# Prompt attention: ScalarE copies the transposed blocks of both heads out of PSUM, in place of VectorE for one head and ScalarE for the other

## The chip, the core and the metric

The kernel runs on one core of a Trainium2 chip. The metric is device time in microseconds (us), the median of several runs. A core has TensorE (PE in the profile; PEld is its weight load), VectorE (DVE), ScalarE (ACT), GpSimd (POOL), and SyncE (SP), which issues all DMAs here. Each engine works through its own instructions in program order; an instruction waits on semaphores for what it needs from the others. Matmuls write to PSUM, and their results are copied from there to SBUF before they can be an operand again.

## The reference, cut to what matters

Two layers of a hybrid encoder, for one prompt of 2048 tokens and 8 short samples. Each layer has an input projection, a state-space branch, a stick-breaking attention branch (8 heads of 64) and an output projection. The change concerns the prompt's attention:

```python
z = jnp.einsum('bqhd,bkhd->bhqk', q, k) * (HEAD_DIM ** -0.5)
mask = k_pos[None, :] < q_pos[:, None]
log_1mb = jnp.where(mask, -jax.nn.softplus(z), 0.0)
after = lax.cumsum(log_1mb, axis=3, reverse=True) - log_1mb
a = jnp.where(mask, jnp.exp(jax.nn.log_sigmoid(z) + after), 0.0)
return jnp.einsum('bhqk,bkhd->bqhd', a, v)
```

## The kernel before

`attn_prompt` runs once in each layer. It loops over blocks of query tiles (four tiles of 128 queries in a block; in layer 1 the last four tiles make two blocks of two, so `nt` is 4 or 2), over four pairs of heads, and over chunks of 512 keys from the diagonal down. For each chunk, head and query tile, TensorE makes the scores `pz` (L819, L820, on the diagonal also the mask, L822), ScalarE takes their sigmoid into `u` (L824), and VectorE runs a cumulative product along the keys (L826, the scan). Then the key blocks of 128 are taken two at a time, as a group: for each block and head TensorE transposes the tiles of `u` into a PSUM bank `pt` (L838), the bank is copied to SBUF as `aT` (L840 for head 0, L841 for head 1), and TensorE multiplies it by the differences of V into `po` (L845). The first L845 of a group waits for the last copy of the group. Where a head pair is done, VectorE makes `za` from `po` (L854).

PSUM holds two `pt` banks while layer 0's attention runs and three in layer 1; of `aT` there are six buffers.

No order is written out by hand: a scheduler takes the whole program, with its own estimate of each instruction's cost, and lays out each engine's order. So attention is interleaved with other work. In layer 0 it runs beside the gated unit `glu`, the modulation matmuls (L242), the output projection (L1246 to L1248) and the input projection of layer 1 (L673 to L675, whose weights ScalarE casts in L171 and VectorE or GpSimd split in L172). In layer 1 it runs beside `glu` and the output projection. In the last microseconds of layer 1's attention that other work has run out.

Counted over the program, 376 banks are copied by each of L840 and L841: 160 pairs in layer 0 and 216 in layer 1, in 188 groups.

Of the kernel before, what the change touches and what calls it, by code (L numbers as in the profile page):

```python
# [44 lines left out]
class Trunk:  # L45
# [731 lines left out]
    def attn_prompt(self, l, blocks):  # L777
        nc = self.nc
        v, gp, sc, pe, ident = nc.vector, nc.gpsimd, nc.scalar, nc.tensor, self.ident
        with ExitStack() as es:  # L780
            ap = self.pool(es, f"a{l}{blocks[0][0]}", right=True)
            for t0, nt, hp in [(t0, nt, hp) for t0, nt in blocks for hp in range(H // 2)]:
# [17 lines left out]
                for kc in range(top, -1, -1):  # L800
                    diag = kc == top
                    nk = (t0 + nt) * 128 - kc * 512 if diag else 512
                    ks = slice(kc * 512, kc * 512 + nk)
                    V1 = ap.tile([128, 4, 128], F32, name="V1", bufs=2)
                    self.dma(V1[:, 0:nk // 128], self.dv_d[l][ks, rp].rearrange("(b p) c -> p b c", p=128))
                    As = [[], []]
                    for hh in range(2):
                        rs = slice(hp * 128 + hh * 64, hp * 128 + hh * 64 + 64)
                        K1 = ap.tile([128, 512], F32R, name="K1", bufs=3)
                        self.dma(K1[:, 0:nk], self.kT[l][rs, :, ks].rearrange("d s t -> (d s) t"))  # L810
                        Q1, Q2 = Qt[hh]
                        for i in range(nt):
                            W = (t0 + i + 1) * 128 - kc * 512 if diag else 512
                            o = 512 - W
                            pz = self.pz()
                            qi = slice(i * 128, (i + 1) * 128)
                            N = max(W, 256)
                            c0, c1 = 512 - N, 512 - N + W
                            pe.matmul(pz[:, c0:512], Q1[:, qi], K1[:, 0:N], start=True, stop=False)  # L819
                            pe.matmul(pz[:, c0:512], Q2[:, qi], K1[:, 0:N], start=False, stop=not diag)  # L820
                            if diag:
                                pe.matmul(pz[:, c1 - 128:c1], self.identb, self.maskb, start=False, stop=True)  # L822
                            u = ap.tile([128, 512], F32, name="u", bufs=16)
                            sc.activation(u[:, o:512], pz[:, c0:c1], AF.Sigmoid, scale=-0.125)  # L824
                            un = u[:, o:512][:, ::-1]
                            v.tensor_tensor_scan(un, un, un, 1.0 if diag else carry[hh * 4 + i], ALU.mult, ALU.bypass)  # L826
                            carry[hh * 4 + i] = u[:, o:o + 1]
                            As[hh].append(u)
                    for j0 in range(0, nk // 128, 2):
                        group = []  # L830
                        for j in range(j0, min(j0 + 2, nk // 128)):
                            i0 = max(0, kc * 4 + j - t0)
                            s = slice(i0 * 128, nq)
                            pTs = [self.pt(), self.pt()]
                            for hh in range(2):
                                for i in range(i0, nt):
                                    off = (512 - ((t0 + i + 1) * 128 - kc * 512)) if diag else 0
                                    pe.transpose(pTs[hh][:, i * 128:(i + 1) * 128], As[hh][i][:, off + j * 128:off + (j + 1) * 128], ident)  # L838
                            aTs = [ap.tile([128, 512], F32, name="aT", bufs=6) for _ in range(2)]
                            v.tensor_copy(aTs[0][:, s], pTs[0][:, s])  # L840
                            last = sc.copy(aTs[1][:, s], pTs[1][:, s])  # L841
                            group += [(j, s, hh, aTs[hh]) for hh in range(2)]
                        for n, (j, s, hh, aT) in enumerate(group):
                            c = slice(hh * 64, hh * 64 + 64)
                            mm = pe.matmul(po[c, s], V1[:, j, c], aT[:, s], start=diag and j == 0,  # L845
                                           stop=kc == 0 and j == 3, tile_position=(0, hh * 64))
                            if n == 0:
                                self.after(mm, last)
# [438 lines left out]
```

## Time and profile before

| | |
|---|---|
| median of 3 runs | 3225.33 us (3224.55 to 3226.41) |
| the profiled execution | 3223.93 us, span 3221.9 us |
| TensorE busy | 92% of the span |
| VectorE busy | 69% |
| ScalarE busy | 40% |
| GpSimd busy | 22% |
| mean granted TensorE clock | 0.965 of full speed |

The profiled execution's own time is 1.4 us below the median; the span is the time from the first to the last instruction in it. Busy shares are means over stages with different limits, so the stages in which the changed lines run matter. A wait is put down to the instruction that ended it, with the engine and tile that released it.

### The profile page before, as it was taken

How to read it: one execution, taken by the hardware profiler on the slowest of the kernel's cores; microseconds unless marked ns; L12 is line 12 of the kernel's file. 1: busy time of each engine (PE TensorE's matmuls, PEld its weight loads, DVE VectorE, ACT ScalarE, POOL GpSimd, SP SyncE). 2: the span in 40 equal slices, each digit the busy share in tenths (PEclk: the TensorE clock that was granted, in tenths of full speed). 3: DMA queues.
4: the chain of work that ended last, by engine and by line, in shares of the span. 5: the costliest groups of instructions: out<-in, count | busy, mean ns of one | idle time of the engine just before them, and what ended most of it. 6: DMA issues, size and time to landing. Idle time of an engine off the chain costs nothing.

```text
span 3221.9 us, 47149 instructions
## 1 busy us (share of the span) xinstructions
PE 2955.8 (92%) x16902; PEld 2268.8 (70%) x16902; DVE 2237.8 (69%) x3885; ACT 1295.2 (40%) x2646; POOL 713.4 (22%) x468
## 2 busy tenths in 40 slices
PE   6978679899988989999999998899999799999998
PEld 4756578798767666767777886677789566666665
DVE  6699774757566667577896637446574889777765
ACT  5632224334442334365443323373243345343432
POOL 1155664101302021221012103312200202111310
PEclk8989899999999999999999998899999899999999
DMA  6645554466677975343434314667764757345552
GB/s 207 169 144 171 207 175 150 134 186 180 227 258 235 300 227 156 111 157 121 130 116 157 129 65 146 228 195 216 229 192 128 240 149 230 116 129 164 188 156 74
DMA packets 516099, 555.27 MB, mean 172 GB/s; under 512 B 87203, under 2 KB 369491, under 8 KB 515098
## 3 DMA queue, kind: packets, MB, share of 16 engines
q1 hardware_dynamic: 515866, 552.26, 54.9%
q8 instruction: 134, 2.20, 0.3%
q14 instruction: 99, 0.81, 0.1%
HBM read 378.12 MB, written 169.86 MB: 170 GB/s over the span
## 4 chain that ended last, share of the span: by engine, by line
PE 61%; DVE 12%; DMA 8%; issue 4%; ACT 2%; SPq 1%; POOL 1%; DVEq 0%; ACTq 0%; POOLq 0%
PE po L845 7%; PE pt L838 7%; PE pm L673 4%; PE pm L674 4%; PE pm L675 4%; PE pz L819 3%; PE pm L1246 3%; PE pm L1247 3%; PE pz L820 3%; PE pm L1248 3%; PE pm L726 3%; DVE u L826 3%; PE pm L728 3%; PE pm L727 3%; PE pz L993 1%
## 5 line engine op out<-in xcount | busy, mean ns | idle before, releaser
L826 DVE TENSOR_TENSOR_SCAN u<-u 128x512 f32<-128x512 f32 (+3 forms) x640 | 723.0, 1166 | 65.6 <-ACT u L824 63.8
L673 PE MATMUL pm<-wH,hH 128*128 128x512 f32 x1088 | 448.9, 413 | 28.8 <-ACT kn L760 16.4
L674 PE MATMUL pm<-wL,hH 128*128 128x512 f32 x1088 | 445.1, 409 | 8.7 <-DVE wL L172 6.9
L675 PE MATMUL pm<-wH,hL 128*128 128x512 f32 x1088 | 445.9, 410 | 4.4 <-POOL hL L649 2.8
L841 ACT COPY aT<-pt 128x512 f32<-128x512 f32 (+1 forms) x376 | 175.5, 470 | 572.8 <-PE pt L838 540.7
L824 ACT ACTIVATE u<-pz 128x512 f32<-128x512 f32 (+3 forms) x640 | 321.8, 536 | 152.5 <-PE pz L820 48.2
L838 PEld LDWEIGHTS pt<-ident,u 128*128 128x128 f32 x2176 | 249.6, 141 | 174.3 <-issue 107.6
L838 PE MATMUL pt<-ident,u 128*128 128x128 f32 x2176 | 340.8, 280 | 26.6 <-DVE aT L840 19.7
L840 DVE COPY aT<-pt 128x512 f32<-128x512 f32 (+1 forms) x376 | 198.9, 533 | 231.0 <-PE pt L838 218.7
L845 PE MATMUL po<-aT,V 128*64 128x512 f32 (+1 forms) x1504 | 285.5, 497 | 12.4 <-DVE za L854 4.6
L819 PE MATMUL pz<-K,Q 128*128 128x512 f32 (+2 forms) x640 | 273.3, 427 | 4.7 <-issue 1.8
L726 PE MATMUL pm<-hH,wH 128*128 128x384 f32 (+1 forms) x768 | 260.9, 340 | 17.5 <-DVE kn L731 17.5
L728 PE MATMUL pm<-hH,wL 128*128 128x384 f32 (+1 forms) x768 | 257.6, 336 | 10.0 <-POOL wL L172 7.9
L673 PEld LDWEIGHTS pm<-wH,hH 128*128 128x128 f32 x1088 | 210.6, 194 | 79.6 <-ACT kn L760 17.5
L727 PE MATMUL pm<-hL,wH 128*128 128x384 f32 (+1 forms) x768 | 258.9, 337 | 0.0
L674 PEld LDWEIGHTS pm<-wL,hH 128*128 128x128 f32 x1088 | 210.6, 194 | 57.4 <-DVE wL L172 10.2
L675 PEld LDWEIGHTS pm<-wH,hL 128*128 128x128 f32 x1088 | 210.7, 194 | 56.9 <-POOL hL L649 6.5
L172 POOL TENSOR_TENSOR wL<-wr,wH 128x512 fp32r<-128x512 f32 x96 | 149.6, 1569 | 422.1 <-ACT wH L171 224.9
L820 PE MATMUL pz<-K,Q 128*128 128x512 f32 (+2 forms) x640 | 235.5, 368 | 0.0
L1246 PE MATMUL pm<-owH,mH 128*128 128x512 f32 x512 | 207.7, 407 | 10.6 <-DVE yt L1249 9.6
L1247 PE MATMUL pm<-owL,mH 128*128 128x512 f32 x512 | 206.2, 403 | 6.2 <-DVE owL L172 5.1
L1248 PE MATMUL pm<-owH,mL 128*128 128x512 f32 x512 | 204.2, 399 | 0.6 <-POOL mL L172 0.6
(373 smaller groups left out, 5245.8 us busy)
## 6 DMA issues: line engine op xcount, KB each, us to landing
wr<-in_w_in_dram SPq DMA_DIRECT2D x192, 256.0 KB
K<-kT SPq DMA_DIRECT2D x184, 256.0 KB
Q<-qT SPq DMA_DIRECT2D x112, 256.0 KB
wm<-in_w_mod_dram SPq DMA_DIRECT2D x24, 1024.0 KB
V<-dv_d SPq DMA_DIRECT2D x92, 256.0 KB
out_dram<-kn SPq DMA_DIRECT2D x68, 256.0 KB
qT<-x SPq DMA_DIRECT2D x64, 256.0 KB
kT<-x SPq DMA_DIRECT2D x64, 256.0 KB
```

The costliest lines, as they stand in the source:

```text
L673: pe.matmul(ps, hH[:, k, cs], wH[k], start=k == 0, stop=False)
L674: pe.matmul(ps, hH[:, k, cs], wL[k], start=False, stop=False)
L675: pe.matmul(ps, hL[:, k, cs], wH[k], start=False, stop=k == KT - 1)
L726: pe.matmul(ps[:, 0:n], wH[k][:, ws], hH[:, k, 0:n], start=k == 0, stop=False)
L727: pe.matmul(ps[:, 0:n], wH[k][:, ws], hL[:, k, 0:n], start=False, stop=False)
L728: pe.matmul(ps[:, 0:n], wL[k][:, ws], hH[:, k, 0:n], start=False, stop=k == KT - 1)
L819: pe.matmul(pz[:, c0:512], Q1[:, qi], K1[:, 0:N], start=True, stop=False)
L820: pe.matmul(pz[:, c0:512], Q2[:, qi], K1[:, 0:N], start=False, stop=not diag)
L824: sc.activation(u[:, o:512], pz[:, c0:c1], AF.Sigmoid, scale=-0.125)
L826: v.tensor_tensor_scan(un, un, un, 1.0 if diag else carry[hh * 4 + i], ALU.mult, ALU.bypass)
L838: pe.transpose(pTs[hh][:, i * 128:(i + 1) * 128], As[hh][i][:, off + j * 128:off + (j + 1) * 128], ident)
L845: mm = pe.matmul(po[c, s], V1[:, j, c], aT[:, s], start=diag and j == 0, stop=kc == 0 and j == 3, tile_position=(0, hh * 64))
```

## The change

One line: the copy of head 0's bank goes to ScalarE, which already copies head 1's.

```diff
                             aTs = [ap.tile([128, 512], F32, name="aT", bufs=6) for _ in range(2)]
-                            v.tensor_copy(aTs[0][:, s], pTs[0][:, s])
+                            sc.copy(aTs[0][:, s], pTs[0][:, s])
                             last = sc.copy(aTs[1][:, s], pTs[1][:, s])
```

The scheduler lays the program out anew. TensorE, GpSimd and SyncE issue the same instructions as before (15256, 473 and 1902; 171 of SyncE's DMAs stand a few places earlier or later), VectorE 376 fewer, ScalarE 376 more. Up to the first attention instruction of layer 0 nothing moves. The last matmuls of other work stand at the same point of layer 1's attention as before.

On VectorE, near the end of layer 1's attention (the scan is printed as SCALAR_TENSOR_TENSOR, L826), before:

```order
L826 SCALAR_TENSOR_TENSOR u<-u 128x384
L840 COPY aT<-pt 128x256
L826 SCALAR_TENSOR_TENSOR u<-u 128x512
L840 COPY aT<-pt 128x256 x4
L826 SCALAR_TENSOR_TENSOR u<-u 128x512 x4
```

and now:

```order
L826 SCALAR_TENSOR_TENSOR u<-u 128x384
L826 SCALAR_TENSOR_TENSOR u<-u 128x512
L826 SCALAR_TENSOR_TENSOR u<-u 128x384
L826 SCALAR_TENSOR_TENSOR u<-u 128x512 x13
L854 SCALAR_TENSOR_TENSOR za<-po,vE,za 128x128 x2
```

The copies that stood four in a row between four scans and the next four are gone, and 13 scans follow each other.

On ScalarE, at the same place (L824 is the sigmoid), before:

```order
L824 ACTIVATE u<-pz 128x512
L841 COPY aT<-pt 128x256 x3
L824 ACTIVATE u<-pz 128x512 x3
L841 COPY aT<-pt 128x256 x2
L824 ACTIVATE u<-pz 128x512
```

and now:

```order
L840 COPY aT<-pt 128x256
L841 COPY aT<-pt 128x256
L840 COPY aT<-pt 128x256
L841 COPY aT<-pt 128x256
L840 COPY aT<-pt 128x256
L841 COPY aT<-pt 128x256
L824 ACTIVATE u<-pz 128x512
L840 COPY aT<-pt 128x256
L824 ACTIVATE u<-pz 128x512 x2
L841 COPY aT<-pt 128x256
```

Head 0's copy stands ahead of head 1's, and in one of the pairs two sigmoids stand between the two.

On TensorE, where the second-to-last head pair ends its diagonal chunk (V_28895 is that chunk's V), before:

```order
L838 MATMUL pt<-ident,u 128x128 x8
L845 MATMUL po<-aT,V_28895 64x256 x4
L838 MATMUL pt<-ident,u 128x128 x2
L845 MATMUL po<-aT,V_28895 64x256 x2
L838 MATMUL pt<-ident,u 128x128 x2
L845 MATMUL po<-aT,V_28895 64x128 x2
```

and now:

```order
L838 MATMUL pt<-ident,u 128x128 x9
L845 MATMUL po<-aT,V_28895 64x256 x4
L838 MATMUL pt<-ident,u 128x128 x5
L845 MATMUL po<-aT,V_28895 64x256 x2
L845 MATMUL po<-aT,V_28895 64x128 x2
```

The four L845 of the second group stood in two runs with transposes between them, and now stand in one. Over the whole order 188 groups stood in 206 such runs, and now in 188.

## Rows read from the trace of the kernel before

**Rows 1.** The page: busy time, share of the span, instructions of each engine.

```profile
PE 2955.8 (92%) x16902; PEld 2268.8 (70%) x16902; DVE 2237.8 (69%) x3885; ACT 1295.2 (40%) x2646; POOL 713.4 (22%) x468
```

**Rows 2.** Stretch, busy us (count): PE, PEld, DVE, ACT, POOL; clock, DMA share, GB/s.

```profile
1030.00:1830.00 800.00, 770.83 (x4446) 557.70 (x4445) 578.91 (x956) 357.78 (x703) 124.98 (x82) 0.99 0.52 164
2570.00:3125.00 555.00, 539.30 (x3006) 380.27 (x3006) 440.40 (x546) 229.72 (x491) 104.27 (x63) 0.99 0.53 161
3125.00:3180.00 55.00, 45.39 (x296) 27.88 (x296) 44.31 (x63) 23.99 (x58) 0.00 (x0) 1.00 0.39 114
```

**Rows 3.** Groups by line and shape: busy us, mean ns | idle ahead, releasers.

```profile
L840 DVE COPY aT<-pt 128x512 f32<-128x512 f32 x172 | 117.3, 683 | 139.4 <-PE pt L838 139.0
L841 ACT COPY aT<-pt 128x512 f32<-128x512 f32 x172 | 100.7, 586 | 298.7 <-PE pt L838 295.9 <-PE pz L822 1.9
...
L840 DVE COPY aT<-pt 128x256 f32<-128x256 f32 x140 | 57.0, 413 | 63.3 <-PE pt L838 56.4 <-PE po L845 6.1
L841 ACT COPY aT<-pt 128x256 f32<-128x256 f32 x140 | 51.9, 378 | 182.3 <-PE pt L838 181.1 <-PE po L845 1.1
```

**Rows 4.** Line L840: who waited for it (us, times).

```profile
  PE pt L838: 19.7, 18
...
  PE po L845: 4.0, 2
```

**Rows 5.** Line L841: who waited for it (us, times).

```profile
  PE pt L838: 4.4, 7
  PE po L845: 3.1, 5
```

**Rows 6.** TensorE's waits, layer 0's attention: us in total, times, longest.

```profile
PE po L845 <- DVE za L854: 3.2, 3, 1.3
```

**Rows 7.** TensorE's waits, layer 1's attention to 3125 us.

```profile
PE pm L1247 <- DVE owL L172: 3.2, 3, 1.6
...
PE pm L1246 <- DVE yt L1249: 2.0, 2, 1.7
PE pt L838 <- DVE u L826: 1.6, 1, 1.6
```

**Rows 8.** TensorE's waits from 3125 to 3180 us.

```profile
PE pt L838 <- DVE aT L840: 8.0, 6, 1.4
```

**Rows 9.** Timeline, 3127 to 3136 us: start, us, engine, instructions [idle before <-releaser].

```profile
3127.87 1.08 PE L845 MATMUL po<-aT,V 128*64 128x256 f32 x8
...
3131.36 0.44 PE L838 MATMUL pt<-ident,u 128*128 128x128 f32 x2 [1.35 <-DVE aT L840]
...
3135.68 1.08 PE L845 MATMUL po<-aT,V 128*64 128x256 f32 x8
...
3127.38 3.61 DVE L826 TENSOR_TENSOR_SCAN u<-u 128x512 f32<-128x512 f32 x3
3130.91 0.73 DVE L840 COPY aT<-pt 128x256 f32<-128x256 f32 x2
...
3133.11 1.58 ACT L824 ACTIVATE u<-pz 128x512 f32<-128x512 f32 x3 [0.85 <-PE pt L838]
3134.56 0.67 ACT L841 COPY aT<-pt 128x256 f32<-128x256 f32 x2
```

**Rows 10.** Timeline, TensorE from 3176 to 3180 us, a group's L845 in two runs.

```profile
3176.77 1.08 PE L845 MATMUL po<-aT,V 128*64 128x256 f32 x8 [0.41 <-DVE za L854]
3177.78 0.44 PE L838 MATMUL pt<-ident,u 128*128 128x128 f32 x2
3178.15 0.65 PE L845 MATMUL po<-aT,V 128*64 128x256 f32 x4
3178.73 0.44 PE L838 MATMUL pt<-ident,u 128*128 128x128 f32 x2
...
3179.47 0.77 PE L838 MATMUL pt<-ident,u 128*128 128x128 f32 x5
```

**Rows 11.** Timeline, ScalarE at 1500 us, inside layer 0's attention.

```profile
1500.34 3.41 ACT L171 CAST wH<-wr 128x512 fp32r<-128x512 f32 x5 [0.16 <-PE pm L675]
```

## The prediction

> **What bounds the kernel now.** I read the page first: TensorE is busy for 92% of the span, VectorE for 69%, ScalarE for 40% [rows 1]. A share over the whole span says little about two stages of the program, so the next view is the busy time of the stretches in which the changed lines run [rows 2]. There TensorE is busy for 771 of 800 us (96%), 539 of 555 us (97%), and, at the end of layer 1's attention, 45.4 of 55 us (83%). VectorE stands at 72%, 79% and 81% in the same stretches, ScalarE at 45%, 41% and 44%. So TensorE bounds all of it, because the scheduler fills attention's gaps with projection matmuls; only in the last stretch, where these have run out, is VectorE nearly as busy as TensorE. The clock granted there is 0.99 to 1.00, so it takes no part.
>
> It follows that this change cannot be worth the work that it takes off VectorE. It can be worth the time in which TensorE stands idle, which is 29 + 16 + 10 us in the three stretches, and of that the part that waits for what the change moves. The view of who waited for a line gives it: TensorE's matmuls waited 19.7 + 4.0 = 23.7 us for VectorE's copies (L840) [rows 4], and 4.4 + 3.1 = 7.5 us for ScalarE's (L841) [rows 5]. There are 376 copies of each, so a copy costs TensorE 63 ns on VectorE and 20 ns on ScalarE. The two do the same job; what differs is the queue that they stand in. The timeline of the last stretch shows it: three scans hold VectorE from 3127.38 for 3.61 us, the two copies behind them start at 3130.91, and the transposes that need the bank start at 3131.36 after 1.35 us of idle [rows 9]. Six such waits make 8.0 us there [rows 8]; the other 15.7 lie scattered over the rest.
>
> **The change part by part.**
>
> *Copies leave VectorE.* Their whole wait goes: -23.7 us. Nothing else can bring it back on VectorE, since no such copy is left there. Below, the bound is 23.7; above, it is this plus what else waits in the same queue, the next term but one.
>
> *Copies join ScalarE.* The duration is no loss: 586 ns against 683 for a bank of 512 columns, 378 against 413 for 256 [rows 3], about 176 us of new ScalarE work for all 376 at the mean of L841. That work takes ScalarE from 45%, 41% and 44% to about 54%, 54% and 63%; the added time of the three stretches is near 76, 73 and 10.5 us, since head 1's banks have the same shapes. All of it lies beside TensorE's work. What counts is the wait per copy, now for 752 copies. Queued behind a copy are the sigmoids, the casts of projection weights and the other head's copy, and TensorE waits for each of these in its turn. The low bound is today's 20 ns each: 752 x 20 = 15.0 us. The high bound is the VectorE price, 63 ns: 47.4 us. I take 25 ns, 18.8 us: near the low end, because ScalarE after the change is less busy than VectorE is today and what stands ahead of a copy is mostly shorter, a sigmoid of about 0.53 us (three in 1.58) in place of a scan of 1.20 (three in 3.61) [rows 9]. One long thing does stand in that queue, five casts that hold it for 3.41 us [rows 11]; head 1's copy already meets them.
>
> *The last stretch by itself.* One round of two groups takes 7.81 us (L845 at 3127.87 and again at 3135.68 [rows 9]). Without the 1.35 us wait it would be 6.46. In one round ScalarE would have four sigmoids, 4 x 0.53, and eight copies at 0.335 (two in 0.67): 2.1 + 2.7 = 4.8 us, and VectorE four scans, 4.8 us. Neither reaches 6.46, so TensorE bounds the round. The order of the change has two sigmoids between the two copies of one pair; 1.1 us later is still inside the round, since TensorE has another group's transposes and two score tiles ahead of the L845 that needs them. So these 8.0 us should go.
>
> *Other work in VectorE's queue.* TensorE also waits for `za`, 3.2 us [rows 6], for `owL`, `yt` and the scan, 3.2 + 2.0 + 1.6 us [rows 7]: 10.0 us together. With 185 us of copies gone ahead of them some come earlier. Bounds 0 and -10; I take -3, as most of such a wait is for the scan or for their own input.
>
> *Runs of L845.* There are 18 runs fewer. In a split group the next transposes start 0.58 us after four matmuls of a run (3178.15 to 3178.73), where eight take 1.01 (3176.77 to 3177.78) and four would take 0.51: 0.07 lost. The two transposes between take 0.37 to L845 (3177.78 to 3178.15); five take 0.77 and two 0.44, so one more is 0.11 and two steps inside a longer run would be 0.22: 0.15 lost [rows 10]. A split costs 0.22 us, 18 of them 4.0: -4 us. The bound on the other side is 0, if a merged group only waits longer for its last copy.
>
> *The last groups,* from 3176 us, have no scans, and there two engines copied side by side. In series the second copy of a pair comes up to 0.34 us later. There are some 11 pairs, most of them covered by the last projection matmuls: +1 us, bounds 0 and +4.
>
> *DMAs.* None is added or removed. In SyncE's order 171 of 1902 stand a few places earlier or later, at most a few entries apart; I price that at nothing, as their landing is covered by double buffers, and give the new order as a whole +-3 us in the range.
>
> The sum is -23.7 + (18.8 - 7.5) - 3 - 4 + 1 = -18.4 us, on the profiled execution's 3223.9: 3205.5. That execution lies 1.4 us under the median, so the forecast for the median is **3207 us**.
>
> The Trainium skill, "Perfetto Trace Analysis", section "Optimizing Scalar/DVE Operations", says that work which either engine can do may go to ScalarE if VectorE is saturated. By that rule the move pays in the last stretch alone, where 81% comes nearest to saturation, and the sum would be -8.0 us, 3217. The waits of rows 4 lie also where VectorE is at 72 and 79%, so I keep the sum by waits.
>
> **The rivals.**
>
> *ScalarE's queue takes over the wait in equal measure.* The wait moves from L840 on VectorE to L840 and L841 on ScalarE. For it speaks that one head's copy now stands behind the other's and both behind sigmoids; against it, that waits of L841 are few today (12 in all [rows 5]). At 45 ns a copy, 752 copies make 33.8 us, and the sum is -23.7 + 26.3 - 3 - 4 + 1 = -3.4: **3222 us**, no change that can be told.
>
> *Copying in series ends the group later: slower.* The mechanism is one: the first L845 of a group waits for the group's last copy, and that is now the fourth on one engine, where it was the second of two on each. The price is the VectorE price for each of 752 copies, 47.4 us, as if ScalarE's queue became what VectorE's is: -23.7 + 39.9 - 3 - 4 + 1 = +10.2, **3235 us**. It decides from (23.7 + 7.5 + 6) / 752 = 49 ns a copy upward. Against it: layer 0 has long stretches of projection matmuls between the last transpose and L845 in the order, so a late copy costs nothing there. For it: layer 0 has two `pt` banks only, so a late copy holds back the next transposes as well. The Trainium skill, "TensorEngine Tiling (Array Packing)", section "PSUM Bottleneck", speaks for this rival: it wants both ScalarE and VectorE for emptying PSUM, which is what the change gives up.
>
> *VectorE was late with more than its copies.* If all 10.0 us of the other waits go too and new waits stay at 20 ns: -23.7 + 7.5 - 10 - 4 = -30: **3195 us**.
>
> **How the numbers follow.** I give my forecast 0.53, the wait that moves over 0.25, the slower rival 0.15, the larger gain 0.07. A measurement of this kernel can tell a difference of about 0.2%, 6.5 us, so faster means under 3218.9 and slower above 3231.8. The forecast's own range is 3197 to 3217 (the waits at 20 to 35 ns a copy, the smaller terms at either bound), nearly all of it faster; with the larger gain and a small part of the second case this makes 0.63 faster. Most of the second case is the same: 0.25. The slower rival less its mild part is 0.12. For 8 in 10 the range reaches from 3194, which holds the larger gain, to 3229, which takes in the case of no change and leaves out most of the slower rival.
>
> **What would show it right or wrong.** Right: TensorE's waits for L840 and L841 together fall from 31.2 to about 19 us, all of them on ScalarE; the round in the last stretch takes near 6.5 us in place of 7.81; VectorE's busy time falls by about 200 us, ScalarE's rises by about 176, and TensorE's stays. Wrong: TensorE's waits for ScalarE's copies at 30 us or more, above all in L845; the round still at 7.8; or idle time of TensorE that goes and comes back in another place, for DMA or for the projection's weights, because the new order put them elsewhere.

## The result and the profile after

The changed kernel is faster by more than was forecast. In the first comparison its median is 3188.6 us (six runs, 3185.51 to 3209.95) against 3224.94 us for the kernel before, ratio 0.9897, 95% interval 0.987 to 0.9925; in a second one (the first experiment) 3199.3 us against 3222.54, ratio 0.9926, interval 0.9903 to 0.995. The forecast was 3207 with a range from 3194 to 3229: the first comparison lies outside it, the second inside. Executions of one kernel spread over some 20 us, so a single profile says where time went only to about 10 us, and the medians decide.

The profiled execution took 3185.51 us. Its page gives the busy time of each engine, which answers to [rows 1]:

```profile
PE 2931.2 (92%) x16902; PEld 2257.7 (71%) x16902; DVE 2067.0 (65%) x3509; ACT 1422.1 (45%) x3022; POOL 715.8 (22%) x468
```

VectorE loses 171 us and ScalarE gains 127, less than the 200 and 176 that the sums of single copies gave, because copies in a row overlap (below). What was not forecast is the first number: TensorE's busy time falls by 24.6 us. Of these, 13.3 us stand ahead of the first score matmul of layer 0's attention (879.56 us before, 866.26 now), where both kernels are the same program, so this part is chance; 12 stand in the stages of attention. The stretches with the same work as in [rows 2], each shifted by what the execution is ahead there (columns as in rows 2):

```profile
1020.00:1820.00 800.00, 776.88 (x4498) 565.84 (x4497) 510.12 (x813) 410.54 (x853) 124.05 (x82) 1.00 0.52 166
2550.00:3087.00 537.00, 528.53 (x2973) 377.70 (x2971) 365.80 (x379) 283.40 (x651) 99.81 (x61) 1.00 0.53 165
3087.00:3142.00 55.00, 50.51 (x331) 31.84 (x329) 34.62 (x33) 33.74 (x93) 1.27 (x1) 1.00 0.42 122
```

In the last of them TensorE is now busy for 50.5 of 55 us (45.4 before), and VectorE has fallen from 44.3 to 34.6. The waits that answer to [rows 4] and [rows 5] are those for line L840 (first fence) and for L841 (second), us and times:

```profile
  PE pt L838: 2.4, 4
  PE po L845: 0.9, 1
```

```profile
  PE pt L838: 5.5, 5
...
  PE po L845: 5.0, 6
```

That is 13.8 us for 752 copies, where 31.2 us stood before and 18.8 were forecast: 18 ns a copy. The durations hold what [rows 3] promised (line and shape, busy us, mean ns):

```profile
L840 ACT COPY aT<-pt 128x512 f32<-128x512 f32 x172 | 101.9, 592 | 34.9 <-PE pt L838 33.1 <-PE po L845 1.3
...
L840 ACT COPY aT<-pt 128x256 f32<-128x256 f32 x140 | 53.6, 383 | 56.9 <-PE pt L838 54.1 <-PE pz L822 2.2 <-PE po L845 0.6
```

The timeline of one round in the last stretch answers to [rows 9]:

```profile
3093.14 1.08 PE L845 MATMUL po<-aT,V 128*64 128x256 f32 x8
...
3095.65 1.08 PE L845 MATMUL po<-aT,V 128*64 128x256 f32 x8
...
3096.67 0.87 PE L838 MATMUL pt<-ident,u 128*128 128x128 f32 x6
...
3097.66 3.64 DVE L826 TENSOR_TENSOR_SCAN u<-u 128x512 f32<-128x512 f32 x3 [1.64 <-ACT u L824]
3097.68 0.50 PE L819 MATMUL pz<-K,Q 128*128 128x512 f32 x1
...
3098.26 0.38 PE L838 MATMUL pt<-ident,u 128*128 128x128 f32 x2
...
3098.75 0.40 ACT L841 COPY aT<-pt 128x256 f32<-128x256 f32 x1
...
3099.00 0.43 ACT L840 COPY aT<-pt 128x256 f32<-128x256 f32 x1
...
3099.59 1.08 PE L845 MATMUL po<-aT,V 128*64 128x256 f32 x8
```

A round takes 6.45 us (3093.14 to 3099.59), as forecast (6.46), and VectorE, which was the late one, now waits 1.64 us for a sigmoid. The reader should notice a second thing: after the six transposes TensorE makes a score (L819 and L820) before the next two transposes, so the banks have time to be emptied. That order is new, and the experiments show what it is worth. (The L841 copy starts at 3098.75 and takes 0.40, the L840 copy starts at 3099.00: two copies in a row overlap by 0.15 us. Over the trace, ScalarE's instructions overlap by 210 us, where they did by 147 before; these 63 us are what its busy time grew less than the sum of the single durations.)

Cut at the same instructions in four profiles (the first L819; the last L1149, of layer 1's state-space branch; the last L726, of its keys' projection; the last L1249, of the output projection, on VectorE; the last L845), the time goes, in us:

| stage | before | before, again | changed | changed, again | mean difference |
|---|---|---|---|---|---|
| ahead of the first score | 1028.6 | 1018.9 | 1020.0 | 1021.3 | (same program) |
| layer 0's attention, to the last L1149 | 996.0 | 1000.3 | 984.0 | 990.9 | -10.7 |
| to the last L726 | 475.7 | 475.7 | 476.8 | 479.7 | +2.6 |
| layer 1's attention, to the last L1249 | 621.3 | 623.9 | 608.5 | 617.2 | -9.8 |
| to the last L845 | 86.1 | 86.1 | 80.2 | 77.4 | -7.3 |
| to the end | 14.2 | 14.2 | 14.2 | 14.2 | 0 |

So some 28 us come from the three stages in which the changed line runs, and 2.6 are lost between them. The last of the three gives 7.3, where 8.0 were forecast. Two profiles of one kernel differ by up to 9 us in a stage of attention.

### The profile page after: what moved, and what is told of

It reads as the page before. It is cut to its first block, busy times and chain, and to the rows that moved or that the text cites. A ratio compares the mean times of both kernels' runs of the same rounds, so it can differ in the third digit from the quotient of the medians.

```text
span 3183.7 us, 47391 instructions
## 1 busy us (share of the span) xinstructions
PE 2931.2 (92%) x16902; PEld 2257.7 (71%) x16902; DVE 2067.0 (65%) x3509; ACT 1422.1 (45%) x3022; POOL 715.8 (22%) x468
## 4 chain that ended last, share of the span: by engine, by line
PE 63%; DVE 9%; DMA 8%; issue 4%; ACT 2%; POOL 1%; SPq 1%; DVEq 0%; ACTq 0%; POOLq 0%
PE po L845 7%; PE pt L838 7%; PE pm L673 4%; PE pm L674 4%; PE pm L675 4%; PE pz L819 4%; PE pz L820 3%; PE pm L1248 3%; PE pm L1247 3%; PE pm L1246 3%; PE pm L726 3%; PE pm L728 3%; PE pm L727 3%; DVE u L826 2%; SPq L163 1%
## 5 line engine op out<-in xcount | busy, mean ns | idle before, releaser
L826 DVE TENSOR_TENSOR_SCAN u<-u 128x512 f32<-128x512 f32 (+3 forms) x640 | 731.1, 1184 | 348.7 <-ACT u L824 347.7
L674 PE MATMUL pm<-wL,hH 128*128 128x512 f32 x1088 | 443.5, 408 | 11.8 <-DVE wL L172 7.3
L824 ACT ACTIVATE u<-pz 128x512 f32<-128x512 f32 (+3 forms) x640 | 323.2, 547 | 78.7 <-PE pt L838 34.5
L838 PEld LDWEIGHTS pt<-ident,u 128*128 128x128 f32 x2176 | 250.1, 141 | 140.7 <-issue 96.3
L838 PE MATMUL pt<-ident,u 128*128 128x128 f32 x2176 | 332.8, 278 | 10.0 <-ACT aT L841 5.5
L841 ACT COPY aT<-pt 128x512 f32<-128x512 f32 (+1 forms) x376 | 178.7, 475 | 362.3 <-PE pt L838 361.3
L845 PE MATMUL po<-aT,V 128*64 128x512 f32 (+1 forms) x1504 | 279.4, 493 | 12.4 <-DVE za L854 6.5
L726 PE MATMUL pm<-hH,wH 128*128 128x384 f32 (+1 forms) x768 | 259.4, 338 | 17.5 <-DVE kn L731 17.5
L819 PE MATMUL pz<-K,Q 128*128 128x512 f32 (+2 forms) x640 | 269.6, 421 | 6.4 <-ACT u L824 3.1
L840 ACT COPY aT<-pt 128x512 f32<-128x512 f32 (+1 forms) x376 | 178.8, 476 | 151.3 <-PE pt L838 115.9
L820 PE MATMUL pz<-K,Q 128*128 128x512 f32 (+2 forms) x640 | 234.9, 367 | 0.0
L1246 PE MATMUL pm<-owH,mH 128*128 128x512 f32 x512 | 208.6, 408 | 11.8 <-DVE yt L1249 8.4
```

Of the source, the lines that this page charges most:

```text
L674: pe.matmul(ps, hH[:, k, cs], wL[k], start=False, stop=False)
L726: pe.matmul(ps[:, 0:n], wH[k][:, ws], hH[:, k, 0:n], start=k == 0, stop=False)
```

## The experiments

**Repeats.** The kernel before and the changed kernel, both unaltered.

> The kernel before once more, with a profile. In the first pair of profiles 8.6 us of the 38.2 us were gained ahead of the first score matmul of layer 0's attention (it started at 1028.6 us before, at 1020.0 us after), where no instruction had moved. Theory A (chance of one execution): the start of that matmul varies between executions of one kernel, so this repeat puts it anywhere from 1019 to 1030 us, and the time stays at 3222 to 3227. Theory B (it belongs to the program): it stands at 1028 to 1029 us again. Forecast: ratio 1.000, 1022 to 1029 us.

> The changed kernel once more, with a profile. Theory A: the first score matmul of layer 0 starts anywhere from 1019 to 1030 us, and what the attention stretches gain (12 us from there to the end of the state-space work at 2004 us, 19 us from 2481 us to the end) stays. Theory B: the first score matmul starts at 1019 to 1021 us again. Time 3186 to 3195, ratio 0.988 to 0.991.

Measured: 3224.52 us (ratio 1.0012, 0.9997 to 1.0026) and 3199.3 (0.9926, 0.9903 to 0.995). The first score starts at 1018.9 and 1021.3 us, where the first pair of profiles had 1028.6 and 1020.0. Theory A holds: the 8.6 us between the first two profiles ahead of any changed instruction were chance. (The 1022 to 1029 us of the first forecast stand for 3222 to 3229.) The changed kernel's repeat misses the 3186 to 3195 us that were expected, and its profile, against the first one of the kernel before, gains less in attention: 5 us to the last L1149 and 13 from the last L726 on, where the first pair had 12 and 19.

**One layer at a time.**

```diff
-v.tensor_copy(aTs[0][:, s], pTs[0][:, s])
+(sc.copy if l == 0 else v.tensor_copy)(aTs[0][:, s], pTs[0][:, s])   # the other run: l == 1
```

> ScalarE copies both heads in layer 0's attention alone; layer 1 as before. Queue theory (the gain is TensorE's wait for copies behind scans): layer 0's stretch gains 9 to 13 us against before, layer 1's nothing; time 3210 to 3216. Rival (the gain is a new order or a better clock somewhere, not the copies of a stage): the gain doesn't split by stage, and this kernel is at 3190 to 3200 or at 3225.

> ScalarE copies both heads in layer 1's attention alone; layer 0 as before. Queue theory: layer 1's stretch gains 15 to 20 us, of it 8 in the end where the projection matmuls have run out (a round of 6.45 us in place of 7.81); time 3204 to 3210. With e3 the gains add up to the change's. Rival: as in e3.

Measured: 3217.59 us for layer 0 (ratio 0.9991, 0.9977 to 1.0005) and 3205.85 for layer 1 (0.9946, 0.9927 to 0.9966). Layer 1 alone gives some 17 us, as expected. Layer 0 alone gives 3 to 5 us, at the edge of nothing, less than the 6 to 12 expected, though its waits for copies fell from 31.2 to 26.7 us; in its profile layer 0's stage is 9 us shorter than in the kernel before (989.0), and the stage behind it 4 us longer (479.9). The two add to about 20 us of the 23 to 36 of the whole change.

**Which engine copies which head.** The engines turned (ScalarE head 0, VectorE head 1), and VectorE for both:

```diff
-v.tensor_copy(aTs[0][:, s], pTs[0][:, s])
-last = sc.copy(aTs[1][:, s], pTs[1][:, s])
+sc.copy(aTs[0][:, s], pTs[0][:, s])            # the other run: v.tensor_copy
+last = v.tensor_copy(aTs[1][:, s], pTs[1][:, s])
```

> Control: ScalarE copies head 0's bank, VectorE head 1's, so each engine has as many copies as before and only the order is new. Queue theory (the gain is the wait for VectorE's queue): no gain, 3219 to 3228 us, TensorE waits about 24 us for VectorE's copies (L841 now) and about 7.5 for ScalarE's, and its busy time stays at about 2952. Rival (the gain comes from the program being laid out anew, whichever engine copies): 3195 to 3212.

> VectorE copies the banks of both heads, ScalarE none. Queue theory at the price of the prediction: 752 copies at 63 ns are 47.4 us in place of 31.2, so 3235 to 3245, all of the wait on VectorE. Rival (the wait per copy grows with what else stands in the queue, since a round of the last stretch then has four scans, 4.8 us, and eight copies, 2.9 us, on VectorE): 3250 or more, and a round of the last stretch of 7.7 us or more. Second rival (one engine for both heads is what helps, since a group then ends in one queue and its L845 stand in one run): under 3215.

Measured: 3208.79 us for the turned engines (ratio 0.9954, 0.994 to 0.9969), and 3272.07 for VectorE alone (1.0146, 1.0131 to 1.0162). For the second the rival's time and its round came in (10.2 us, L845 at 3184.80 and 3195.02), but not its reason: the waits for copies are 49.9 us, 66 ns a copy, so the price did not grow, and they explain 19 of the 48 us. TensorE's busy time in the three stages of attention is 23 us higher (2041.0, where the kernel before has 2015.7 and 2020.9), and its clock was granted at the lower level, 1.2 GHz, for 118 us there, in place of 61 and 75. The first contradicts the queue theory outright. It was meant as a control, and it gained 15 us while TensorE waited longer for copies:

```profile
  PE pt L838: 9.0, 5
```

for L840 on ScalarE, and for L841 on VectorE

```profile
  PE po L845: 19.5, 17
...
  PE pt L838: 12.8, 12
```

41.3 us in all, where the kernel before had 31.2. Its gain stands where no copy is: between the last L1149 and the last L726, before and with the turned engines (columns as in rows 2):

```profile
2024.60:2500.30 475.70, 452.11 (x2727) 370.65 (x2719) 259.19 (x577) 200.68 (x417) 86.33 (x74) 0.98 0.64 198
```

```profile
2037.30:2496.80 459.50, 447.89 (x2727) 370.28 (x2719) 255.88 (x577) 201.02 (x417) 85.28 (x74) 0.99 0.65 205
```

TensorE is idle for 11.6 us there in place of 23.6. The three stages of attention together take 1709.5 us, no less than in the kernel before (1703.4 and 1710.3). A new order of the whole program is worth 15 us by itself, with no copy taken off VectorE.

**Whole runs of L845.** The copies of before; the first L845 of a group waits for VectorE's last copy too, so that there are 188 runs in place of 206.

```diff
-v.tensor_copy(aTs[0][:, s], pTs[0][:, s])
+first = v.tensor_copy(aTs[0][:, s], pTs[0][:, s])
...
-    self.after(mm, last)
+    self.after(mm, last); self.after(mm, first)
```

> The kernel before, copies on both engines, where the first L845 of a group waits for VectorE's last copy too, so the L845 stand in 188 runs, as in the changed kernel, in place of 206. Prediction's price (18 splits at 0.22 us): -4 us, 3217 to 3222, copies' waits about 31 us as before. Theory 2 (TensorE's busy time fell by some 13 us because runs are whole): 3209 to 3215 with busy time at about 2940. Rival (a whole run waits longer for the later copy): 3223 or more, with more than 31 us of waits for copies.

Measured: 3223.12 us, ratio 0.9997 (0.9987 to 1.0006). The waits for copies are 36.5 us, 5.3 more, and TensorE's busy time 2962.9 is not less than before. So the term comes to nothing on balance. Whether whole runs save busy time that the longer waits take back is not shown: in this profile (3235.08 us, 12 above the median) the clock of 1.2 GHz was granted for 89 us in attention's stages, in place of 61 and 75.

**TensorE's order held.** To part the engine from the order, TensorE's instructions were chained in a given order (each may only be issued behind the one before it; no wait for its end), and the rest was left to the scheduler. Three kernels: ScalarE's copies in the order of before, the copies of before in the order of the changed kernel, and the turned engines in the order of before.

```diff
+for p, n in zip(names, names[1:]):     # TensorE's instructions, in the order wanted
+    tc.add_manual_dep(n, p.name, mybir.DependencyInfo(mybir.DependencyClass.NoSync, ...), reason="order")
```

> ScalarE copies both heads, as in the changed kernel, but TensorE's instructions are held to the order in which they stand in the kernel before. Queue theory (the gain is the wait for copies): most of the gain is left, 3200 to 3212 us, waits for copies near 14 us. Order theory (the gain is that TensorE's work stands in another order): 3218 to 3228.

> VectorE copies head 0 and ScalarE head 1, as before, but TensorE's instructions are held to the order of the changed kernel. Queue theory: no gain, since the copies stand behind the scans as before, 3218 to 3235 us, with 31 us of waits for copies or more. Order theory: most of the gain is there, 3195 to 3208.

> ScalarE copies head 0 and VectorE head 1, TensorE held to the order of the kernel before. Without that hold the same swap gained 15 us while the waits for copies rose from 31 to 41. If that gain is the order's, it is gone here: 3220 to 3232. If it belongs to which head is copied by which engine (the copy that ends the group's wait is now on VectorE), it stays: 3204 to 3214.

In the traces TensorE's order is that of the kernel before, or of the changed one, instruction by instruction. The medians decide here: the profiled execution of the first took 3228.49 us, 13 above its median, and that of the second 3221.65, 15 below. Measured, with the two kernels themselves:

| | TensorE in the order of before | in the order of the changed kernel |
|---|---|---|
| VectorE and ScalarE copy | 3224.94, 3224.52 us | 3236.97, ratio 1.0041 (1.0026 to 1.0056) |
| ScalarE copies both | 3215.05, ratio 0.9975 (0.9961 to 0.9989) | 3188.6, 3199.3, ratios 0.9897, 0.9926 |

Neither theory stands alone: the first run lies between its two forecasts, the second 2 us above both. With the order held, ScalarE's copies give 0.25%, about 8 us; the new order by itself costs 0.41%, about 13 us; together they give 0.74 to 1.03%. The turned engines in the order of before take 3238.43 us (1.005, 1.0031 to 1.0068), and TensorE waits 68.6 us for copies: their gain was the order's too.

The waits show the same. ScalarE's copies in the old order, line L840 and then L841:

```profile
  PE pt L838: 9.0, 15
...
  PE po L845: 0.4, 1
```

```profile
  PE pt L838: 8.1, 15
...
  PE po L845: 2.7, 4
```

20.2 us, or 27 ns a copy, in many short waits of the transposes. But TensorE waits 39.8 us for VectorE's other results in the three stages of attention, where the kernel before has 31.6 and 31.0: in the old order, what the copies no longer cost comes back in part elsewhere. (This execution took 3228.49 us, 13 above the median.) The copies of before in the new order make the waits for VectorE's (L840) longer than in [rows 4]:

```profile
  PE pt L838: 28.7, 21
...
  PE po L845: 2.5, 1
```

A round of the last stretch lets the reader see why. ScalarE's copies, old order:

```profile
3132.32 1.08 PE L845 MATMUL po<-aT,V 128*64 128x256 f32 x8
...
3135.62 0.87 PE L838 MATMUL pt<-ident,u 128*128 128x128 f32 x6
...
3136.91 0.44 PE L838 MATMUL pt<-ident,u 128*128 128x128 f32 x2 [0.41 <-ACT aT L840]
3137.10 0.48 PE L819 MATMUL pz<-K,Q 128*128 128x512 f32 x1
...
3138.16 0.44 PE L838 MATMUL pt<-ident,u 128*128 128x128 f32 x2 [0.34 <-ACT aT L841]
...
3139.46 1.08 PE L845 MATMUL po<-aT,V 128*64 128x256 f32 x8
```

Copies of before, new order:

```profile
3125.01 1.08 PE L845 MATMUL po<-aT,V 128*64 128x256 f32 x8
...
3128.61 0.44 PE L838 MATMUL pt<-ident,u 128*128 128x128 f32 x2 [1.25 <-DVE aT L840]
...
3132.82 1.08 PE L845 MATMUL po<-aT,V 128*64 128x256 f32 x8
```

The round takes 7.81 us before, 7.14 with ScalarE's copies alone, 7.81 with the new order alone, and 6.45 with both. In the old order two transposes follow straight on the six and wait 0.41 us for ScalarE to empty the bank, and the next two 0.34; the new order puts score matmuls there. With VectorE's copies that helps nothing: the wait of their round stands in the other group, 1.25 us behind the scans.

**VectorE kept busy.** The changed kernel with 376 added copies on VectorE that nobody waits for. In a first form they write to a new tile:

```diff
+v.tensor_copy(junk[:, s], As[0][nt - 1][:, 512 - nq + i0 * 128:512])
```

> The changed kernel, with a copy on VectorE beside each pair (376, from u into a tile that nothing reads), so that VectorE keeps the number of instructions that it had and no engine waits for the added ones. Theory 1 (the gain is the wait for the copies themselves): 3192 to 3200 us as the changed kernel, waits for VectorE's other work as in the changed kernel. Rival (a relieved VectorE is early with its scans, za, yt and splits, and that is a good part of the gain): 3205 to 3218, with more of TensorE's waits for za, u, yt and owL than in the changed kernel.

Measured: 3256.09 us, ratio 1.0091 (1.0076 to 1.0106), slower than both theories allow. The trace shows why it decides nothing: the new tile moved the program, the last L1149 ends at 1851.9 us, where it ends between 2004 and 2070 in the other kernels. So the second form writes into a tile that exists, and TensorE is held to the order of the changed kernel:

```diff
+v.tensor_copy(self.last[:, 0:min(256, n)], As[0][nt - 1][:, 512 - min(256, n):512])   # n = nq - i0 * 128
```

> The changed kernel with TensorE held to its own order, and a copy of at most 256 columns on VectorE beside each pair (376, about 0.37 us each, from u into a tile that is written over later), for which no other engine waits. Theory 1 (only the wait for the copies counts): as the changed kernel, 3192 to 3202 us. Rival (VectorE relieved is early with its scans and za, and a good part of the gain is that): 3206 to 3225, and TensorE waits more for u, za and the sigmoids that need a free u.

Measured: 3216.42 us, ratio 0.9984 (0.997 to 0.9998): most of the gain is gone, though the waits for copies are 13.6 us, as in the changed kernel, and the round of the last stretch is still 6.45 us (L845 at 3125.69 and 3132.14). The added work is this, busy us and mean ns:

```profile
L841 DVE COPY last<-u 128x256 f32<-128x256 f32 x340 | 121.6, 358 | 6.4
...
L841 DVE COPY last<-u 128x128 f32<-128x128 f32 x36 | 10.0, 278 | 0.6
```

In the three stages of attention, TensorE waits 42.8 us for VectorE's other results (`yt`, `za`, splits, the scan), where it waits 25.7 and 28.4 us in the changed kernel's two profiles and 31.6 and 31.0 in those of the kernel before. In the traces TensorE, ScalarE and GpSimd run the changed kernel's order instruction by instruction, and VectorE too but for the added copies and two instructions that moved, so it is the added work that costs. The rival holds for this order: a good part of the gain needs a relieved VectorE. In the order of before relief alone did not do it (the 39.8 us above).

**Two turns that change no work.** Whether the changed kernel's order is a rule or a draw: two turns of the writing order, applied to both kernels.

```diff
-<copy of head 0>; last = <copy of head 1>
+<copy of head 1>; <copy of head 0>                          # first turn
-group += [(j, s, hh, aTs[hh]) for hh in range(2)]
+group += [(j, s, hh, aTs[hh]) for hh in (1, 0)]             # second turn
```

`last` stays ScalarE's last copy.

> The kernel before, with the two copies of a pair written in the other order (head 1's first); the engines are those of before. Theory 1 (an order fits the engines that it was laid out for, any order about as well): within 8 us of the kernel before, 3215 to 3231. Theory 2 (the order of the kernel before is an unlucky one, and any other is better): 3195 to 3212, as for the swapped heads.

> The changed kernel with the two copies written in the other order, head 1's first. Theory 1: 3185 to 3205 us, as the changed kernel. Theory 2 (the order of the changed kernel is a lucky one): 3207 to 3225, most of the gain gone.

> The kernel before, with L845 of head 1 written ahead of head 0's in each group. Theory 1: within 8 us of the kernel before, 3215 to 3231. Theory 2: 3195 to 3212.

> The changed kernel, with L845 of head 1 written ahead of head 0's. Theory 1: 3185 to 3205. Theory 2: 3207 to 3225.

| | copies by both engines | by ScalarE | difference |
|---|---|---|---|
| as written | 3224.94, 3222.54 | 3188.6, 3199.3 | -36, -23 |
| copies turned | 3284.51 (1.0193, 1.0162 to 1.0224) | 3230.9 (1.0022, 1.0007 to 1.0037) | -54 |
| L845 turned | 3222.43 (0.9992, 0.9979 to 1.0005) | 3208.26 (0.9944, 0.9925 to 0.9962) | -14 |

With L845 turned, the kernel before follows theory 1 and the changed kernel theory 2; with the copies turned, both are slower than either theory allows. ScalarE's copies win in each of the three pairs, as they did in both held orders (three pairs alone would fall so by chance one time in eight). They halve TensorE's waits for copies in each: from 31.2 and 30.2 us to 13.8 and 15.4, from 53.0 to 26.4, from 35.6 to 15.1. But the size of the gain runs from 14 to 54 us, and a turn alone moves the kernel before by up to 61 us and the changed one by up to 42: the changed kernel as written has the best of its three orders, and with its copies turned it is no faster than the kernel before as written. The slowest, the kernel before with its copies turned, has its L845 in 268 runs. With the changed kernel's copies turned, the transposes wait again, mostly for L840, which is head 1's copy there, written first though its bank is filled last:

```profile
  PE pt L838: 19.6, 30
...
  PE po L845: 2.5, 1
```

## Why the prediction was wrong

The direction and the mechanism were right: the waits for L840 and L841 fell, from 31.2 and 30.2 us to 13.8 and 15.4, and are all on ScalarE. The sum by waits was near, too: in attention's three stages TensorE's idle time fell by 15.8 us on the mean of two profiles each, where its sum was 18.4. The size of the whole was not right. **The step that failed is the pricing of the new order**, where the prediction says "give the new order as a whole +-3 us in the range", and with it that TensorE's busy time "stays". It took the order of before as given, summed the waits that an engine takes away, and treated the rest as a small disturbance. The runs put the new order at +13 us with the copies of before and at 16 to 26 us of gain with ScalarE's (3215.05 against 3199.3 and 3188.6), and TensorE's busy time in attention fell by 12.0 us. Point by point:

- *Copies leave VectorE*, -23.7: right, no wait for it is left there.
- *Copies join ScalarE*, 25 ns a copy: right for the order in which it was worked out, 27 ns (20.2 us over 752) with that order held. With the new order it is 18 ns, 20 in the repeat. A term is missing beside it: TensorE's waits for ScalarE's other results (sigmoids, casts) rose from 9.9 and 12.4 us to 17.7 and 15.2 in attention's stages.
- *The last stretch*, round 6.46 us and -8.0: measured 6.45 and -7.3, but for half another reason. ScalarE's queue gives 0.67 us a round, the new order with it 0.69.
- *Other work in VectorE's queue*, -3: by the waits -4.2 (31.3 to 27.1, means of two profiles), so near. But the 10.0 us that it started from were a third of the 31.6 that TensorE waits for VectorE's other results in attention's three stages. The two largest, in the kernel before, are (us, times, longest)

```profile
PE pm L1246 <- DVE yt L1249: 9.6, 5, 3.3
PE pm L1192 <- DVE gHc L171: 7.0, 1, 7.0
```

  and of these it counted 2.0. And the copies that left VectorE were 198.9 us, not 185. Yet 132 us of work put back on VectorE cost 17 to 28 us (3216.42 against 3199.3 and 3188.6), with the copies' waits unchanged. The order of the changed kernel counts on an early VectorE. The rival "VectorE was late with more than its copies", given 0.07 and 3195 us, came nearest to the time, by luck in part: of the 10.0 us that it lets go, the waits show 4.2.
- *Runs of L845*, -4: nothing on balance in the run that made them whole.
- The forecast's own range, "3197 to 3217 (the waits at 20 to 35 ns a copy, the smaller terms at either bound)", does not follow from its terms, which give 3195 to 3224 at their bounds.
- TensorE's busy time, "stays", and the clock, which "takes no part": both wrong. In the three stages of attention the busy time fell from 2015.7 and 2020.9 us to 2003.4 and 2009.3. Two groups of lines carry most of it; in the repeat of the kernel before

```profile
L838 PE MATMUL pt<-ident,u 128*128 128x128 f32 x2176 | 342.6, 282 | 24.9 <-DVE aT L840 19.8 <-ACT aT L841 2.4 <-DVE u L826 1.2
L845 PE MATMUL po<-aT,V 128*64 128x512 f32 (+1 forms) x1504 | 287.1, 499 | 13.1 <-DVE za L854 4.6 <-DVE aT L840 4.0 <-ACT aT L841 4.0
```

and in the changed kernel

```profile
L838 PE MATMUL pt<-ident,u 128*128 128x128 f32 x2176 | 332.8, 278 | 10.0 <-ACT aT L841 5.5 <-ACT aT L840 2.4 <-DVE u L826 1.9
L845 PE MATMUL po<-aT,V 128*64 128x512 f32 (+1 forms) x1504 | 279.4, 493 | 12.4 <-DVE za L854 6.5 <-ACT aT L841 5.0 <-ACT aT L840 0.9
```

The idle time before L838 falls by 14.9 us, and the busy time of the same 2176 transposes by 9.8. Most of the 12.0 us goes with the clock. In the records of the clock, the level of 1.2 GHz was granted in these stages for 61 and 75 us in the kernel before and for 38 and 55 in the changed kernel. Layer 1's attention in the kernel before, again, and in the changed kernel (columns as in rows 2, the clock third from the end):

```profile
2494.90:3118.80 623.90, 590.77 (x3279) 418.39 (x3279) 500.72 (x621) 254.20 (x548) 114.57 (x65) 0.98 0.56 171
```

```profile
2480.80:3089.30 608.50, 585.67 (x3297) 419.44 (x3297) 428.12 (x450) 313.50 (x725) 118.21 (x65) 0.99 0.57 176
```

Between two executions of one program, 14 and 17 us more at that level go with 5.2 and 5.9 us more of busy time. At that rate the 22 us less are an estimated 8 of the 12.0. Nor is it in these four profiles alone: over all executions the mean granted clock is 0.966 to 0.968 in each set of the kernel before, 0.971 and 0.970 in the two of the changed kernel. Whether it is cause or effect of the shorter time was not tested: the turned engines, at 0.967, gained 15 us without it. The other 4 us of busy time stay open; the held orders lie between (2011.7 for ScalarE's copies in the old order, 2008.7 for the copies of before in the new one).

The slower rival (copies in series end the group later) decides from 49 ns a copy; 18 to 27 were measured. With the copies turned it was 26.4 us or 35 ns, and that kernel, at 3230.9 us, is still no faster than the kernel before: TensorE waits there for ScalarE's other results for 25.0 us and for DMAs for 25.6, where the kernel before has 9.9 and 9.5. The Trainium skill, "TensorEngine Tiling (Array Packing)", section "PSUM Bottleneck", wants both engines for emptying PSUM, where the copy may have become the bottleneck. Here TensorE bounds, busy for 92%, and the advice, taken without that condition, would have chosen wrongly: one engine did better than two in all three pairs and with the order held, provided it is ScalarE; VectorE alone lost 1.46%. The rule of the Trainium skill's "Perfetto Trace Analysis", section "Optimizing Scalar/DVE Operations", that such a move pays where VectorE is saturated, would have left the gain to the last stretch (-8.0 us); that stretch gave 7.3, and the stages in which VectorE stood at 72 and 79% gave 10.7 and 9.8 in the profiles (for layer 0, changed alone, the medians show only 3 to 5).

What stays open is how much of the 14 to 54 us is ScalarE's as a rule, how much the order's and how much the clock's. Three orders are too few to say, and an order cannot be read as good or bad from its waits for copies alone: the turned engines waited 41.3 us for copies and were 15 us faster than the kernel before with 31.2.

## What to carry to other kernels

Where a scheduler lays the program out, an edit has two prices, the engine's and the new order's; in this kernel the second was as large as the first, so a forecast from waits needed a range of that size, and a control that changes the order alone (a turn of two independent lines) shows what it is. Here it paid to move a copy out of a queue in which long instructions stand, even though the other engine then does it twice in series. Work that nobody waits for was not free on an engine whose other results are waited for.

## What the runs showed of the hardware that was not expected

The work ahead of the first score, which no kernel here changes, took from 1018.0 to 1032.1 us in the eighteen profiles. The granted clock goes with it. Windows from the start to the first score, of the repeat of the kernel before, and of the run with whole L845:

```profile
0.00:1018.90 1018.90, 869.15 (x5004) 713.65 (x5005) 729.39 (x1493) 395.83 (x798) 341.85 (x217) 0.94 0.61 189
```

```profile
0.00:1032.10 1032.10, 880.96 (x5005) 722.81 (x5006) 726.97 (x1493) 395.69 (x798) 341.70 (x217) 0.93 0.60 187
```

TensorE's busy time there differs by 11.8 us of the 13.2, at a mean granted clock of 0.94 and 0.93. In the records of the clock, the level of 1.2 GHz was granted for 116 us ahead of the first score in the one and for 154 us in the other; over the eighteen profiles that time and the start of the first score have a correlation of 0.78.
